# RWKV recurrence of a two-layer diffusion step: a product of 128 columns split into 64x64 parts, and a new order of the work

## The chip, the cores and the metric

The kernel runs on one core of a Trainium2 chip. A core has five engines that work in parallel, each through its own instructions in order: TensorE (PE, matrix products; PEld is its loading of weights), VectorE (DVE), ScalarE (ACT), GpSimd (POOL) and SyncE (SP), which here mostly issues DMAs. The metric is the device time of one execution in microseconds. Three runs of the kernel before gave 3995.91, 4006.51 and 4013.2 us; the median is 4006.51 us.

## The reference

One inference step over 128 context tokens and 2048 latent tokens of width 1024, in two layers. Layer 0 is Fourier mixing beside neighbourhood attention. Layer 1 is a bidirectional RWKV-7 mixer: 16 heads of 64, each with a 64x64 state, once forward and once backward, then a norm, a gate and an output projection. The recurrence is what the change touches:

```python
def step(S, inp):
    r_t, w_t, k_t, v_t, kk_t, a_t = inp
    sa = jnp.einsum('ebhvk,ebhk->ebhv', S, kk_t)
    S = (S * w_t[..., None, :] - sa[..., None] * (kk_t * a_t)[..., None, :]
         + v_t[..., None] * k_t[..., None, :])
    return S, jnp.einsum('ebhvk,ebhk->ebhv', S, r_t)
```

The output is the two token streams, the context keys and values of layer 0, and the final states of the context.

## The kernel before

The phases run one after the other: projections, Fourier mixing, attention and output of layer 0, projections of layer 1, then `phase_rwkv`, and `Final`, which norms, gates and projects row tiles of 128 tokens. The Tile framework derives the semaphores; in `phase_rwkv` the order of instructions on every engine is the order in which the program names them (`manual_schedule`).

The recurrence does not go token by token. It takes chunks of 64 tokens in a form with a triangular system per chunk and head. A **window** `w` (17 of them) holds four **units** `u`: two chunks forward (u = 0, 1) and two backward (u = 2, 3). Window 0 is the context. Eight pairs of heads lie in the tiles, one head in partitions 0 to 63, the other in 64 to 127 (`HF[0]`, `HF[1]`).

The work of a window is cut into 196 operations (some with instructions on one engine, the DMA ones on SP), named after small functions. `RW_PLAN` lists them once, each as `lag.name.arguments`; the loop at the end of `phase_rwkv` runs through this list again and again, and an entry with lag 3 works on the window three rounds back. So the list is one round of a software pipeline over up to five windows, and it sets the order on every engine's queue.

The operations that the prediction speaks of, with their engines and lines:

- `hl`, `ld`, `vl` (SP): loads of inputs; `ld` brings three tiles of 256 KB for a unit, `vl` the values. `st`, `sb` (SP): stores.
- `la` (PE, L1165), then `lt`, `lh`, `lf` (ACT, L1177, L1179, L1187, L1192): decay and rate.
- `sc` (DVE scan, L1201), `ew`, `ei` (ACT exponentials, L1205, L1209), `wc` (POOL, L1213).
- `fk`, `th_`, `bb`, `bk`, `xa`, `xr`, `fr` (DVE, L1218 to L1253): the tiles `BKb` (b and k) and `Xb` (r~ in columns 0 to 63, the other operand in 64 to 127). `bd` (SP, L1233): copies b of the upper heads beside their k, so that columns 64 to 191 of the upper half hold k and b.
- `ps` (PE): two loops. The first (L1265) makes [b k] x r~, the second (L1269) [b k] times the other operand. Each fills one of two buffers `pq` of PSUM, two banks each, that `la`, `ps`, `pt`, `pb`, `p1` and `p2` use in turn (`grab`).
- `dr` (DVE, L1276) masks the first result, `dx` (DVE, L1281) and `al` (ACT copy) take the second; `ad` (SP, L1295) moves halves of what `al` wrote. `pt` (PE transposes, L1303) with `at` (ACT); `pb` (PE, L1313) with `ab` (ACT).
- `tl` (DVE, L1327), 31 steps `td` (two DVE instructions each, L1339 and L1340), `tu`, `tt` (DVE, L1344, L1348), `tm` (POOL memset): the 32x32 triangles, inverted for a whole window at once. Then `uc` (ACT), `p1` (PE, L1360), `m1` (ACT), `p2` (PE, L1372), `uv` (ACT) put together the 64x64 inverses `UB`.
- per chunk `j` of the window and direction `e`: `RV` (PE, L1398), `R` (L1407), `rc` (ACT), `Z` (PE, L1426), `zc` (ACT), `S` (PE, L1442), `sa` (DVE sum into the state, L1447), `sm` (DVE decay of the state, L1455), and for the output `W_` (PE, L1419), `Y` (L1468), `yo` (ACT).

Arguments are the unit (`ps.3`) or chunk and direction (`sa.0.1`).

Three more tables hang other work into this order. `RW_FILL` says before which operations, counted from the first, steps of `z_gate` run: the second half of layer 1's gate product, 17 tiles of nine steps, 153 in all. `RW_LATE` is the operation before which the buffers of that product are given back. `RW_END` and `RW_TAIL` count from the end of the 3332 operations: at `RW_END` buffers are closed, and `RW_TAIL` says before which operations steps of `Final` run, `w` for loading and splitting the output weights (a split is one ACT and one DVE instruction a chunk), `t` for the first row tile, `u` for preparing the second.

Of the kernel before, what the change touches and what calls it, by code (L numbers as in the profile page):

```python
# [921 lines left out]
def z_gate(nc, g, hh, w, g2, zp, pp):  # L922
# [71 lines left out]


def phase_rwkv(tc, g, ins, outs, final):
# [23 lines left out]
    with ExitStack() as es:  # L1020
# [234 lines left out]
        def blocks(t):  # L1255
            return t.rearrange("p x (k t) -> p x k t", t=64)

        @op
        def ps(w, u):

            e, m, iW, t, f, BK, X = parts(w, u)
            o, q = blocks(grab(("ps", u, 0))), blocks(grab(("ps", u, 1)))
            for p in range(KC):
                for h in range(2):
                    nc.tensor.matmul(o[:, h, p], BK[HF[h], p, 64 * h:64 * h + 128], X[HF[h], p, 0:64], start=True, stop=True)  # L1265
            for p in range(KC):
                for x in range(2):
                    for h in range(2):
                        nc.tensor.matmul(q[HF[h ^ x], x, p], BK[HF[h], p, 64 * x:64 * x + 64], X[HF[h], p, 64:128],  # L1269
                                         start=True, stop=True)  # L1270
# [215 lines left out]
        with tc.manual_schedule():  # L1486
# [346 lines left out]
```

## Time and profile before

| | us |
|---|---|
| profiled execution, its time | 4006.46 |
| its span in the profile | 4004.7 |
| median of three runs | 4006.51 |
| PE busy, whole span | 3509.4 (88%) |
| DVE busy | 2597.0 (65%) |
| ACT busy | 1730.1 (43%) |
| POOL busy | 782.3 (20%) |
| first and last matmul of `ps` start | 2301.7, 3593.2 |

Times in the profile are microseconds from the start of the span. "Busy" counts the union of an engine's instructions, so a group of pipelined matmuls has a busy time far below its count times the duration of one. An idle time in a row is put down to what ended it last ("<-DVE OM L1276": the engine stood until that instruction had finished). The granted clock is the share of full speed that TensorE's throttle let through. A product of F32 operands appears as two matmul instructions.

### The profile page before, as it was taken

What the parts mean: (1) busy time and instruction counts of PE and PEld (TensorE: products, weight loads), DVE (VectorE), ACT (ScalarE), POOL (GpSimd) and SP (SyncE); (2) the same over time, 40 slices, a digit from 0 to 9 for tenths busy, and PEclk for the clock granted to TensorE, in tenths of its full rate; (3) what the DMA queues carried; (4) which work ended last, traced back from release to release, by engine and by line L of the source; (5) the groups of instructions that cost most, each with busy time, mean ns of one, the idle gap of its engine ahead of it and who ended that gap; (6) DMA issues with size and microseconds to landing.
All of it is one profiled execution on the core that took longest, in us unless ns stands there. A gap on an engine that the chain in (4) does not pass through costs nothing. (4 is left out here: it accounts for less than half of the span.)

```text
span 4004.7 us, 93003 instructions
## 1 busy us (share of the span) xinstructions
PE 3509.4 (88%) x39520; PEld 3039.7 (76%) x39520; DVE 2597.0 (65%) x4364; ACT 1730.1 (43%) x3629; POOL 782.3 (20%) x434
## 2 busy tenths in 40 slices
PE   6999998889999979999899997888888888885677
PEld 3999997567777769888687776877888778884555
DVE  6201101478867765899862347877878878875997
ACT  5110011266645533544442344555565555543444
POOL 3000000332202223323332320000000000001665
PEclk8999998999999989999899997788778888787888
DMA  6122214565546742434315542333233233224543
GB/s 213 64 71 86 69 58 139 159 172 143 135 121 191 186 111 81 135 103 115 119 67 153 157 122 79 88 92 86 78 92 86 78 92 98 76 76 152 202 165 115
DMA packets 514383, 463.07 MB, mean 116 GB/s; under 512 B 217111, under 2 KB 420391, under 8 KB 512430
## 3 DMA queue, kind: packets, MB, share of 16 engines
q1 hardware_dynamic: 506350, 444.95, 38.1%
q10 hardware_dynamic: 7616, 12.16, 0.9%
q8 instruction: 310, 5.08, 0.5%
q14 instruction: 107, 0.88, 0.1%
HBM read 314.13 MB, written 129.48 MB: 111 GB/s over the span
## 5 line engine op out<-in xcount | busy, mean ns | idle before, releaser
L34 POOL TENSOR_TENSOR xl<-xt,xh 128x1792 fp32r<-128x1792 f32 (+4 forms) x64 | 246.8, 3867 | 487.8 <-ACT xh L30 244.3
L40 PE MATMUL p<-ul,wh 128*128 128x436 f32 (+1 forms) x800 | 291.7, 365 | 2.4 <-DVE ul L34 2.1
L38 PE MATMUL p<-uh,wh 128*128 128x436 f32 (+1 forms) x800 | 291.5, 365 | 0.0
L39 PE MATMUL p<-uh,wl 128*128 128x436 f32 (+1 forms) x800 | 289.7, 362 | 0.0
L819 DVE SCALAR_TENSOR_TENSOR xt<-s,l1s,xt 128x448 f32<-128x448 f32 (+4 forms) x256 | 246.8, 1016 | 46.7 <-ACT xt L818 46.7
L834 PE MATMUL p<-xh,w 128*128 128x448 f32 (+2 forms) x640 | 240.4, 376 | 17.7 <-ACT w L30 10.2
L1213 POOL COPY WC<-W 128x8 f32<-128x8 f32 x68 | 29.8, 438 | 1133.4 <-DVE Sc L1455 671.4
L835 PE MATMUL p<-xh,w 128*128 128x448 f32 (+2 forms) x640 | 239.7, 374 | 0.0
L30 ACT ACTIVATE xh<-xt 128x1792 fp32r<-128x1792 f32 (+4 forms) x64 | 99.8, 1570 | 226.7 <-DVE xt L819 107.0
L1265 PE MATMUL pq<-Xb,BKb 64*128 64x64 f32 x2176 | 162.5, 304 | 37.6 <-DVE OM L1276 28.2
L1340 DVE TENSOR_TENSOR xe<-xe,l1s 128x31 f32<-128x31 f32 (+15 forms) x527 | 180.8, 343 | 18.1
L1339 DVE TENSOR_TENSOR l1s<-xe,xe 128x31 f32<-128x31 f32 (+15 forms) x527 | 179.6, 341 | 16.4
L1265 PEld LDWEIGHTS pq<-Xb,BKb 64*128 64x128 f32 x2176 | 151.2, 215 | 46.8 <-DVE OM L1276 31.0
L818 ACT ACTIVATE xt<-u,l1s 128x448 f32<-128x448 f32 (+4 forms) x256 | 142.0, 625 | 61.5 <-POOL xl L34 46.0
L40 PEld LDWEIGHTS p<-ul,wh 128*128 128x128 f32 x800 | 151.8, 190 | 12.6 <-DVE ul L34 4.5
L38 PEld LDWEIGHTS p<-uh,wh 128*128 128x128 f32 x800 | 151.9, 190 | 7.8 <-ACT uh L30 0.3
L39 PEld LDWEIGHTS p<-uh,wl 128*128 128x128 f32 x800 | 152.1, 190 | 7.5
L34 DVE TENSOR_TENSOR wl<-w,wh 128x2048 fp32r<-128x2048 f32 x12 | 27.5, 2291 | 189.5 <-ACT wh L30 189.5
L832 PE MATMUL p<-xl,w 128*128 128x448 f32 (+2 forms) x640 | 148.4, 369 | 1.1 <-POOL xl L34 1.1
L434 POOL TENSOR_TENSOR kl<-ld,kh 128x1088 fp32r<-128x1088 f32 x16 | 42.2, 2659 | 547.8 <-ACT kh L433 547.5
L834 PEld LDWEIGHTS p<-xh,w 128*128 128x128 f32 x640 | 123.6, 193 | 32.5 <-ACT w L30 11.1
L1303 PE MATMUL pq<-ident,BKb 64*128 64x64 f32 x1088 | 62.0, 256 | 92.0 <-DVE OM L1276 44.8
(375 smaller groups left out, 10036.9 us busy)
## 6 DMA issues: line engine op xcount, KB each, us to landing
x<-x SPq DMA_DIRECT2D x34, 512.0 KB
zu<-u1T SPq DMA_DIRECT2D x34, 512.0 KB
kk<-kkC SPq DMA_DIRECT2D x68, 256.0 KB
k<-kC SPq DMA_DIRECT2D x68, 256.0 KB
r<-rC SPq DMA_DIRECT2D x68, 256.0 KB
sv<-v SPq DMA_DIRECT2D x136, 128.0 KB
x<-in_x_sample SPq DMA_DIRECT2D x32, 512.0 KB
wmod<-in_ada_w SPq DMA_DIRECT2D x16, 1024.0 KB
```

Source lines behind the costliest of these rows:

```text
L34: (eng or nc.vector).tensor_tensor(lo, x, hi.bitcast(F32), op=ALU.subtract)
L38: nc.tensor.matmul(out, ah, bh, start=start, stop=False)
L39: nc.tensor.matmul(out, al, bh, start=False, stop=False)
L40: nc.tensor.matmul(out, ah, bl, start=False, stop=stop)
L818: nc.scalar.activation(x[:, j], us[hh][:, j, 1:n + 1], AF.Copy, scale=mu1[:, i, k:k + 1])
L819: nc.vector.scalar_tensor_tensor(x[:, j], ss[hh][:, j, :n], muh[:, i, k:k + 1], x[:, j], op0=ALU.mult, op1=ALU.add)
L832: nc.tensor.matmul(p[:, :n], w(wh, k), xl[:, k, :n], start=False, stop=(k == KC - 1))
L834: nc.tensor.matmul(p[:, :n], w(wh, k), xh[:, k, :n], start=(k == 0), stop=False)
L835: nc.tensor.matmul(p[:, :n], w(wl, k), xh[:, k, :n], start=False, stop=False)
L1265: nc.tensor.matmul(o[:, h, p], BK[HF[h], p, 64 * h:64 * h + 128], X[HF[h], p, 0:64], start=True, stop=True)
L1339: nc.vector.tensor_tensor(t, L[:, m:, j:m].to_broadcast([P, n, m]), Tm[:, j:m, :m].to_broadcast([P, n, m]), op=ALU.mult)
L1340: nc.vector.tensor_tensor(o, o, t, op=ALU.subtract)
```

## The change

The first loop of `ps` multiplied, for each pair of heads and each half, a stationary block of 64 rows and 128 columns (b and k side by side; the upper half starts 64 columns later, at k, so that its output rows come out as k, then b). Now it takes b and k apart as blocks of 64 columns and sends each to the half of the output where the 128-column form had put it. The numbers computed are the same. The order of the four products of a pair of heads goes over four combinations of row half and output half, as in the second loop. It no longer reads the columns that `bd` copies; `pt` still does.

The tables are replaced. All 196 operations are in both plans, and the plan has another starting point in its round (some operations that stood first with lag 4 now stand last with lag 3). `tl` stands last, with lag 2, in place of first, with lag 3. `RW_FILL` spreads its 153 steps up to operation 147 instead of 124.

```diff
--- before.py
+++ after.py
@@ -971,25 +971,25 @@
 
 
 RW_RINGS = 7, 6
-RW_FILL = {0: 20, 1: 1, 2: 1, 3: 1, 4: 1, 5: 1, 6: 1, 7: 2, 
...
-RW_END = -50
-RW_TAIL = {-50: 'wwtw', -46: 'w', -32: 'wwwwwttwtt', -31: 'twt', -30: 'ttw', -29: 't', -28: 'tt', -27: 'uw', -25: 'tt', -23: 'twtt', -22: 't', -20: 'uwt', -12: 'ttuwtttuwtt', -11: 'tuwt', -8: 'ttuwtttu', -2: 'tt'}
-RW_LATE = 126
+RW_FILL = {0: 20, 1: 1, 2: 1, 3: 1, 4: 1, 5: 1, 7: 1, 
...
+RW_END = -49
+RW_TAIL = {-29: 'wwtwwwwwwwttwtttwtt', -25: 'tw', -13: 'tttwutttwt', -12: 'ttwutttwutttwutttwut', -11: 'tt', -9: 'wutt', -1: 'tutt'}
+RW_LATE = 149
 RW_PLAN = """
-    3.tl 3.td.0 2.ei.1 4.rc.1.0 3.td.1 4.Z.1.0 4.yo.0.1 3.td.2 4.W_.1.0 3.td.3 3.td.4 3.td.5 4.rc.1.1 3.td.6 3.td.7
-    2.ps.0 3.td.8 3.td.9 3.td.10 4.Z.1.1 2.ld.2 4.zc.1.0 2.xr.1 2.al.0 4.Y.1.0 4.st.0.1 2.dr.0 4.W_.1.1 3.td.11 3.pt.3
-    2.dx.0 3.td.12 2.bk.1 4.st.0.0 2.bb.1 4.zc.1.1 4.Y.1.1 3.vl.0.0 2.fr.1 4.S.1.0 3.td.13 2.pt.0 4.yo.1.0 4.sa.1.0
-    3.RV.0.0 2.xa.1 3.at.3 2.ld.3 2.bd.1 3.td.14 3.td.15 4.S.1.1 2.ad.0 3.td.16 2.at.0 2.la.2.0 2.la.2.1 2.lt.2.0
-    2.lh.2.0 3.td.17 2.lt.2.1 4.sm.1.0 4.sa.1.1 3.RV.0.1 2.pt.1 2.lh.2.1 3.td.18 3.td.19 3.td.20 3.td.21 3.td.22
-    3.td.23 3.td.24 3.td.25 3.R.0.0 2.pb.1 2.at.1 2.wc.1 3.W_.0.0 3.vl.1.0 3.td.26 2.ab.1 3.td.27 3.td.28 3.td.29
-    1.hl.0 2.lf.2.1 3.td.30 3.tu 3.tt 2.ps.1 3.uc 3.sb.3 2.dr.1 2.sc.3 3.rc.0.0 2.lf.2.0 4.sm.1.1 3.p1 2.al.1 2.sc.2
-    2.ew.2 2.wc.2 2.dx.1 2.fk.3 3.m1 2.xr.2 2.xa.2 2.th_.2 3.R.0.1 4.yo.1.1 2.ei.2 2.th_.3 2.ew.3 3.p2 2.bb.2 2.ei.3
-    1.la.0.0 2.bb.3 2.bk.3 3.W_.0.1 2.wc.3 2.fk.2 3.rc.0.1 4.st.1.1 3.uv 1.lh.0.0 3.Z.0.0 2.bk.2 2.fr.2 1.lt.0.0
-    3.Z.0.1 3.zc.0.0 2.bd.3 2.ad.1 2.fr.3 2.xa.3 1.hl.2 2.xr.3 1.ld.1 2.pb.3 2.ab.3 1.la.0.1 1.ld.0 3.S.0.0 2.bd.2
-    3.sa.0.0 4.st.1.0 3.zc.0.1 2.pt.2 1.lt.0.1 1.sc.0 3.S.0.1 3.Y.0.1 3.vl.1.1 2.tm 3.sa.0.1 1.lh.0.1 2.at.2 3.RV.1.0
-    2.ps.3 1.ew.0 1.lf.0.1 3.RV.1.1 1.sc.1 1.lf.0.0 2.al.3 1.ei.0 3.sm.0.0 1.xr.0 1.xa.0 2.dx.3 2.dr.3 2.ps.2 1.th_.0
-    3.Y.0.0 3.R.1.0 2.al.2 1.fk.0 1.th_.1 2.ad.3 3.sm.0.1 1.fk.1 3.R.1.1 1.bb.0 1.wc.0 2.ad.2 1.bd.0 1.ew.1 1.bk.0
-    3.yo.0.0 2.vl.0.1 2.dx.2 2.sb.1 1.fr.0 2.dr.2
+    3.td.0 3.td.1 4.st.0.1 3.td.2 3.td.3 4.st.0.0 3.td.4 4.Y.1.0 3.td.5 3.at.3 3.td.6 2.ps.0 3.td.7 2.al.0 3.td.8
+    3.td.9 3.td.10 3.sb.1 4.yo.1.0 4.Y.1.1 2.dr.0 4.S.1.0 4.S.1.1 3.td.11 2.dx.0 3.td.12 3.vl.0.0 3.td.13 2.pt.0
+    4.sa.1.0 2.xa.1 2.bb.1 2.la.2.1 2.fr.1 3.td.14 3.td.15 2.at.0 3.td.16 3.td.17 3.RV.0.0 2.bd.1 2.la.2.0 3.td.18
+    2.lt.2.1 4.sm.1.0 2.xr.1 3.R.0.0 3.vl.0.1 3.W_.0.0 3.td.19 2.lh.2.1 3.rc.0.0 4.sa.1.1 3.sb.3 3.td.20 3.td.21
+    3.td.22 2.lh.2.0 3.td.23 3.td.24 2.pb.1 3.td.25 2.lt.2.0 2.ab.1 3.td.26 3.td.27 4.yo.1.1 3.td.28 3.vl.1.0 2.pt.1
+    2.at.1 3.td.29 3.td.30 3.tu 3.RV.0.1 3.tt 2.ps.1 2.tm 2.wc.1 2.dr.1 2.lf.2.1 4.sm.1.1 2.lf.2.0 2.ld.3 2.sc.2
+    2.al.1 3.uc 2.ld.2 2.ew.2 2.sc.3 3.p1 3.R.0.1 3.m1 2.ei.2 3.rc.0.1 2.th_.2 4.st.1.0 2.dx.1 2.xr.2 2.fk.2 2.wc.2
+    3.p2 2.ad.0 2.xa.2 2.ew.3 2.bk.2 2.fk.3 2.ei.3 2.th_.3 2.bb.3 1.la.0.0 2.wc.3 2.bb.2 3.W_.0.1 4.st.1.1 3.uv 2.fr.2
+    2.bk.3 3.Z.0.1 2.fr.3 3.Z.0.0 2.pb.3 1.lh.0.0 2.bd.2 1.lt.0.0 3.zc.0.1 2.xr.3 1.la.0.1 3.zc.0.0 2.ab.3 1.lt.0.1
+    2.xa.3 1.hl.2 3.S.0.1 1.ld.0 3.sa.0.1 3.S.0.0 2.bd.3 1.lh.0.1 3.sa.0.0 2.pt.2 1.sc.0 3.Y.0.1 2.at.2 3.RV.1.0
+    1.sc.1 3.sm.0.0 1.ew.0 1.ld.1 2.ps.3 2.ad.1 1.lf.0.1 3.vl.1.1 3.RV.1.1 1.xa.0 1.xr.0 1.wc.0 1.lf.0.0 2.dr.3 0.hl.0
+    2.dx.3 3.sm.0.1 1.th_.0 1.th_.1 2.al.3 1.ei.0 1.fk.0 2.ps.2 3.Y.0.0 3.yo.0.1 1.ew.1 1.fk.1 2.ad.3 2.dx.2 1.bb.0
+    2.al.2 3.R.1.1 2.ad.2 1.bd.0 3.yo.0.0 2.dr.2 3.rc.1.1 3.R.1.0 3.rc.1.0 1.bk.0 1.ei.1 3.Z.1.1 2.pt.3 3.Z.1.0 1.fr.0
+    3.W_.1.0 3.zc.1.0 3.zc.1.1 2.tl 3.W_.1.1 1.bk.1
 """
 
 
@@ -1261,8 +1261,9 @@
             e, m, iW, t, f, BK, X = parts(w, u)
             o, q = blocks(grab(("ps", u, 0))), blocks(grab(("ps", u, 1)))
             for p in range(KC):
-                for h in range(2):
-                    nc.tensor.matmul(o[:, h, p], BK[HF[h], p, 64 * h:64 * h + 128], X[HF[h], p, 0:64], start=True, stop=True)
+                for x in range(2):
+                    for h in range(2):
+                        nc.tensor.matmul(o[HF[h ^ x], h, p], BK[HF[h], p, 64 * x:64 * x + 64], X[HF[h], p, 0:64], start=True, stop=True)
             for p in range(KC):
                 for x in range(2):
                     for h in range(2):
```

More of the change, by code (lines that the diff above doesn't have):

```diff
@@ L973 @@
 RW_RINGS = 7, 6
-RW_FILL = {0: 20, 1: 1, 2: 1, 3: 1, 4: 1, 5: 1, 6: 1, 7: 2, 8: 1, 9: 1, 10: 1, 11: 1, 12: 1, 13: 1, 14: 1, 15: 1, 16: 1, 17: 1, 18: 1, 19: 1, 20: 1, 21: 2, 22: 1, 23: 1, 24: 1, 25: 1, 26: 1, 27: 1, 28: 1, 29: 1, 30: 1, 31: 1, 32: 1, 33: 1, 34: 1, 35: 2, 36: 1, 37: 1, 38: 1, 39: 1, 40: 1, 41: 1, 42: 1, 43: 1, 44: 1, 45: 1, 46: 1, 47: 1, 48: 1, 49: 2, 50: 1, 51: 1, 52: 1, 53: 1, 54: 1, 55: 1, 56: 1, 57: 1, 58: 1, 59: 1, 60: 1, 61: 1, 62: 1, 63: 2, 64: 1, 65: 1, 66: 1, 67: 1, 68: 1, 69: 1, 70: 1, 71: 1, 72: 1, 73: 1, 74: 1, 75: 1, 76: 2, 77: 1, 78: 1, 79: 1, 80: 1, 81: 1, 82: 1, 83: 1, 84: 1, 85: 1, 86: 1, 87: 1, 88: 1, 89: 1, 90: 2, 91: 1, 92: 1, 93: 1, 94: 1, 95: 1, 96: 1, 97: 1, 98: 1, 99: 1, 100: 1, 101: 1, 102: 1, 103: 1, 104: 2, 105: 1, 106: 1, 107: 1, 108: 1, 109: 1, 110: 1, 111: 1, 112: 1, 113: 1, 114: 1, 115: 1, 116: 1, 117: 1, 118: 2, 119: 1, 120: 1, 121: 1, 122: 1, 123: 1, 124: 1}
@@ L975 @@
-RW_END = -50
-RW_TAIL = {-50: 'wwtw', -46: 'w', -32: 'wwwwwttwtt', -31: 'twt', -30: 'ttw', -29: 't', -28: 'tt', -27: 'uw', -25: 'tt', -23: 'twtt', -22: 't', -20: 'uwt', -12: 'ttuwtttuwtt', -11: 'tuwt', -8: 'ttuwtttu', -2: 'tt'}
-RW_LATE = 126
+RW_FILL = {0: 20, 1: 1, 2: 1, 3: 1, 4: 1, 5: 1, 7: 1, 8: 1, 9: 1, 10: 1, 11: 1, 12: 1, 13: 1, 14: 1, 15: 1, 17: 1, 18: 1, 19: 1, 20: 1, 21: 1, 22: 1, 23: 1, 24: 1, 25: 1, 26: 1, 28: 1, 29: 1, 30: 1, 31: 1, 32: 1, 33: 1, 34: 1, 35: 1, 36: 1, 38: 1, 39: 1, 40: 1, 41: 1, 42: 1, 43: 1, 44: 1, 45: 1, 46: 1, 47: 1, 49: 1, 50: 1, 51: 1, 52: 1, 53: 1, 54: 1, 55: 1, 56: 1, 57: 1, 59: 1, 60: 1, 61: 1, 62: 1, 63: 1, 64: 1, 65: 1, 66: 1, 67: 1, 68: 1, 70: 1, 71: 1, 72: 1, 73: 1, 74: 1, 75: 1, 76: 1, 77: 1, 78: 1, 80: 1, 81: 1, 82: 1, 83: 1, 84: 1, 85: 1, 86: 1, 87: 1, 88: 1, 89: 1, 91: 1, 92: 1, 93: 1, 94: 1, 95: 1, 96: 1, 97: 1, 98: 1, 99: 1, 101: 1, 102: 1, 103: 1, 104: 1, 105: 1, 106: 1, 107: 1, 108: 1, 109: 1, 110: 1, 112: 1, 113: 1, 114: 1, 115: 1, 116: 1, 117: 1, 118: 1, 119: 1, 120: 1, 122: 1, 123: 1, 124: 1, 125: 1, 126: 1, 127: 1, 128: 1, 129: 1, 130: 1, 131: 1, 133: 1, 134: 1, 135: 1, 136: 1, 137: 1, 138: 1, 139: 1, 140: 1, 141: 1, 143: 1, 144: 1, 145: 1, 146: 1, 147: 1}
```

## The prediction

> **What bounds the kernel now.** I read the page first: TensorE is the busiest engine and the recurrence (L1265 and its neighbours) is its most broken-up stage. Then the stage by itself. A window of the recurrence begins with one VectorE transpose (`tl`, L1327), so its starts give the period.
>
> ```profile
> L1327 DVE STREAM_TRANSPOSE xe<-AF x17: 1917/1952/1973, 2415.3 to 3596.9; 128x1024 f32<-128x1024 f32 x17
> ```
> Seventeen starts, 16 intervals between 2415.3 and 3596.9: 73.85 us a window. Next the busy time by stretch: first the start up to the first `tl`, then window 0, then thirteen whole windows, then 103 us from the last `tl` on. The columns are stretch, length, busy us (instructions) of PE, PEld, DVE, ACT and POOL, granted clock, DMA share, GB/s.
>
> ```profile
> 2302.00:2415.30 113.30, 101.77 (x821) 78.64 (x820) 49.74 (x69) 44.59 (x94) 26.61 (x17) 0.95 0.42 117
> 2415.30:2488.90 73.60, 56.84 (x1164) 53.66 (x1166) 57.41 (x111) 36.41 (x82) 2.65 (x5) 0.67 0.24 66
> 2566.30:3526.20 959.90, 815.09 (x20395) 771.16 (x20391) 775.95 (x1469) 534.21 (x1171) 36.38 (x78) 0.83 0.31 87
> 3596.90:3700.00 103.10, 62.45 (x1289) 55.85 (x1284) 59.89 (x105) 38.73 (x75) 10.34 (x4) 0.73 0.47 143
> ```
> In the thirteen windows (73.84 us each) PE is busy 62.7 us a window, DVE 59.7, ACT 41.1, POOL 2.8. PE leads, yet idles 11.1 us a window and DVE 14.2; neither is full, so I ask who waits for whom. The waits of DVE over the same thirteen windows (us in total, times, longest):
>
> ```profile
> DVE Sc L1447 <- PE pz L1442: 113.0, 24, 8.0
> DVE Xb L1281 <- ACT AF L1134: 23.1, 13, 1.8
> DVE BKb L1228 <- issue: 7.9, 13, 2.1
> ```
> DVE waits 8.7 us a window for the sum into the state (`sa`, L1447), 1.8 for the mask of the second product (`dx`, L1281) and 0.6 before `bb`. One window's DVE, with the stalls in brackets, shows where:
>
> ```profile
> 2899.75 1.19 DVE L1276 TENSOR_TENSOR OM<-pq,masks 128x1024 f32<-128x1024 f32 x1
> ...
> 2920.49 0.69 DVE L1447 TENSOR_TENSOR Sc<-pz,Sc 128x512 f32<-128x512 f32 x1 [7.44 <-PE pz L1442]
> ...
> 2924.10 0.69 DVE L1447 TENSOR_TENSOR Sc<-pz,Sc 128x512 f32<-128x512 f32 x1 [1.52 <-PE pz L1442]
> ...
> 2929.79 0.69 DVE L1281 TENSOR_TENSOR Xb<-pq,masks 128x512 f32<-128x512 f32 x1 [1.78 <-ACT AF L1134]
> ...
> 2938.39 1.97 DVE L1327 STREAM_TRANSPOSE xe<-AF 128x1024 f32<-128x1024 f32 x1
> ```
> From its `tl` to the transpose before 2899.75 and on to the first `sa` DVE runs without a stall worth naming. It stands 7.44 us before that `sa`, 1.52 before the other direction's `sa`, 1.78 before `dx` of unit 3, and then works on to the next `tl`. So DVE's own row of work plus these three holes makes the period. What PE does in that stretch:
>
> ```profile
> 2894.02 3.36 PE L1265 MATMUL pq<-Xb,BKb 64*128 64x64 f32 x32
> 2897.32 1.98 PE L1269 MATMUL pq<-Xb,BKb 64*64 64x64 f32 x64
> 2900.99 3.62 PE L1360 MATMUL pq<-xe,AF 32*32 32x32 f32 x128 [1.69 <-DVE OM L1276]
> 2904.54 1.97 PE L1407 MATMUL pz<-Sc,Xb 64*64 64x64 f32 x32
> 2906.44 3.62 PE L1372 MATMUL pq<-UB,M 32*32 32x32 f32 x128
> 2909.99 2.08 PE L1165 MATMUL pq<-hb,wa 64*128 64x128 f32 x16
> 2912.00 1.97 PE L1419 MATMUL py<-Sc,Xb 64*64 64x64 f32 x32
> 2913.76 2.55 PE L1426 MATMUL pz<-R,UB 64*64 64x64 f32 x64
> 2916.24 1.96 PE L1313 MATMUL pq<-srk,f 128*128 128x16 f32 x16
> 2918.13 1.16 PE L1165 MATMUL pq<-hb,wa 64*128 64x128 f32 x16
> 2919.22 1.15 PE L1442 MATMUL pz<-sv,OM 128*64 128x64 f32 x32
> ...
> 2922.26 0.71 PE L1303 MATMUL pq<-ident,BKb 64*128 64x64 f32 x15 [1.69 <-DMA BKb<-BKb]
> ...
> 2926.00 2.00 PE L1265 MATMUL pq<-Xb,BKb 64*128 64x64 f32 x32
> 2927.93 1.16 PE L1269 MATMUL pq<-Xb,BKb 64*64 64x64 f32 x64
> ```
> The 7.44 us are a chain: the mask at 2899.75 frees the bank that `p1` (L1360) fills, then `p2` (L1372), `W_` (L1419), `Z` (L1426), `pb`, `la`, and `S` (L1442) at 2919.22, whose result `sa` adds. No `ps` is in that chain. The 1.52 us are the second `S` standing in PE's queue behind a transpose (`pt`, L1303) that waits 1.69 us for a DMA into BKb. The 1.78 us are `ps` of unit 3, 2926.00 to 2929.1, followed by ACT's copy (`al`), which L1281 waits for.
>
> **The matmuls.** Per unit 16 products of 64 rows x 128 columns become 32 of 64x64. F32 products count twice in the rows, so 32 instructions become 64, and in the run 2176 become 4352. The second loop of the same function already runs 4352 of 64x64 on the same four parts in the same order:
>
> ```profile
> L1265 PE MATMUL pq<-Xb,BKb 64*128 64x64 f32 x2176 | 162.5, 304 | 37.6 <-DVE OM L1276 28.2 <-DVE xe L1276 5.8 <-DMA BKb<-BKb 3.5
> ...
> L1269 PE MATMUL pq<-Xb,BKb 64*64 64x64 f32 x4352 | 95.1, 248 | 0.0
> ```
> Busy time per instruction: 162.5/2176 = 74.7 ns against 95.1/4352 = 21.9 ns. The new loop differs from the second one only in its banks and in which half of X moves, so I give it the second loop's 95.1 us: PE sheds 67.4 us in the run, 4.0 us a window. At the fast clock a unit goes from 2.00 to 1.16 us, at the slow one from 3.36 to 1.98. Bounds: from 95.1 (nearest row) up to 162.5 (if using both column halves of one bank from one row half cost what 128 columns cost).
>
> One rule speaks against that price. The Trainium skill (TensorE: Matmul & The Clock Gate, section "Wait — 56ns, not 53.3ns?") says that matmuls never start closer than about 25 ns, however short; by it, as an estimate, the new loop would take 109 us and the saving would be 54 us instead of 67. The trace disagrees: 64 of them take 1.16 us, 18 ns each.
>
> What of the 4.0 us lies on DVE's path? Only unit 3's `ps` ends a DVE hole, so at an unchanged order 0.84 of the 1.78 us goes; `ps` of unit 1 ends (2899.3) before its mask can begin anyway (2899.75, after a DVE transpose), and units 0 and 2 delay nobody. The rest becomes PE idle time.
>
> **The order.** I wrote out the new plan per engine, from `tl` round to `tl`.
>
> DVE: between `tl` and the transposes that end `td` the operations are the same ones (`xr.1` later, `bk.1` earlier). Between there and the first `sa` they are again the same nineteen. So the first hole, which is the chain above minus these nineteen, keeps its size if the chain does; in the chain PE still has `p1, R, p2, la, W_, Z, Z, pb, la, S`, only with direction 1 ahead of direction 0. I leave 7.44 as it is.
>
> After that: the two `S` now stand next to each other, and `pt.2` behind both; its DMA `bd.2` is issued on SP ahead of the six unit loads instead of behind them. The hole of 1.52 goes. The second `S` takes 1.15 us after the first, `sa` itself 0.69, so up to 0.5 of it may come back. The two scans follow both sums, covering `Y`, `RV` and `ps.3` on PE. Then `dr.3` comes before `dx.3`, and `al.3` after it. `dr.3` needs only the first, now shorter, half of `ps.3`, and `dx.3` starts a 1.2 us mask later, with no copy ahead of it: the hole of 1.78 goes. What is late next? `tl`, which waits for the last `ad` DMA; `al.2` now stands behind `yo.0.1` and `ew.1` on ACT, but `ps.2` starts earlier since its bank comes free with the earlier `dr.3`. I take no stall, with up to 1.8 (as much as the hole removed) as the bad end.
>
> Other queues: on SP `ld.2` and `ld.3` move behind the `td` stretch and their first users (`th_.2`, `fk.3`) come a few DVE operations behind; on POOL `wc.1` moves behind the memset `tm`, and `ew.2` waits for it; on ACT `lf.2.x` and `al.1` move ahead of `uc`. POOL has 2.8 us of work a window and ACT 41.1 of 73.8, so each has cover; without it `ew.2` would push the chain. PE receives `Z.1` and `pt.3` before `tl`, off DVE's path.
>
> Sum of a window: 1.5 + 1.8, plus half of the 0.6 before `bb`, which now has `dx.2` ahead of it: 3.6 us less, 70.2 us. Ends: 0.84 (only the shorter `ps`) and 5.0. Over 16 intervals: 58 us, ends 13 and 80.
>
> **Start.** The gate product of layer 1 fills PE there, nine steps a tile, in this spacing:
>
> ```profile
> 2290.24 1.02 PE L968 MATMUL pg<-zg,zs 128*128 128x512 f32 x2
> ...
> 2296.59 0.59 PE L968 MATMUL pg<-zg,zs 128*128 128x512 f32 x1
> ```
> 6.35 us a tile is 0.71 us a step. All 153 steps stand before the first `tl` now; 139 will. The other 14 (9.9 us) fall into window 0's `td`, where PE is busy 56.84 of 73.60 us: its 16.8 idle us hide them, and if that cover fails they cost their 9.9 there. With four `ps` at 0.84 the start sheds 13.3 us of PE work, and PE is 90% busy there (101.77 of 113.30). I take 10, ends 0 and 13.
>
> **End.** The output weights' first step moves from 50 to 29 operations before the last one, from about `p1` to after `RV.1.0`, some 21 us later (2904.5 to 2926 in the window shown). Five weight splits, each waiting for a load, now stand in DVE's queue ahead of the last window's `sm.0.1`; before, they and a row tile's first steps stood ahead of `sa.0.1`, so one detour replaces another. DVE idles 43 of the 103 us there, which covers a shift; I take 0, ends -10 and +21.
>
> Sum: 58 + 10 + 0 = 68 us off the profiled execution's own 4006.46 (its span of 4004.7 and 1.8 around it), which stands at the median of the runs, 4006.51: **3938 us**, with an own range of 3915 to 3965.
>
> **Rivals.**
> *PE bounds the window.* Its 85% is the largest share, and then all 67.4 us come off whatever the order: 3939 us. Against it: the largest DVE hole holds no `ps`. The time can't tell it from the forecast; the holes can. 0.06.
>
> *The first hole shrinks too.* In the window shown the chain ran mostly at the slow clock: `R` and `W_` take 1.97 us each, against 1.15 for the 32 instructions of L1442 at 2919.22, and the first `la` 2.08 against 1.16 for the second. With most of that gone, 2 us less in every window, 32 more: 3906 us. For it: the clock changes from window to window. Against: nothing in the edit touches that stretch. 0.09.
>
> *A new wait eats the order's gain.* `tl` waits for `ad.2`, or the second `sa` for PE, as much as now; only 0.84 us a window and the four `ps` of the start are left, 13 + 3 = 16 us: 3990 us. For it: every operation there is moved, and the queues are in order. 0.13.
>
> *The clock falls: slower.* Less PE work in the same period means more idle, and a lower clock: window 0 has PE busy 77% at clock 0.67, the thirteen 85% at 0.83. L1265's mean of 2.39 us a unit (162.5/68) lies 29% of the way from 2.00 to 3.36. So the changed PE work, 58.7 us a window, would be 48.8 at the fast clock and, 1.7 times that, 83 at the slow one. At half slow it is 66 us; with the 11.1 us that PE idles now, 77, 3.2 more than now, 51 in the run; less 10 at the start: 4047 us. It decides above 41% slow, where PE's work passes the present 62.7. Against it: with the period at 70.2 PE is 84% busy, as now. 0.07.
>
> The Trainium skill (the same page, section "Why this matters for your kernels") says that one window of idling of over about 3 us sends the array back to half clock. By that, too, longer PE holes would make this last case. The trace has stretches of both speeds, 3.36 and 2.00 us for the same 32 instructions, and does not show what starts them.
>
> **How the numbers follow.** Forecast 0.65, the rivals 0.06, 0.09, 0.13, 0.07. The range reaches from the deeper hole to the eaten gain: 3905 to 3988, leaving out the clock and about half of the eaten gain. A measurement of this kernel tells about 0.5%, 20 us, from no change. The eaten gain lies on that line, so of its 0.13 I count 0.05 as faster and 0.08 as same: faster 0.85, same 0.08, slower 0.07.
>
> **What would show it.** Right: L1269 and the new line near 95 us each; `tl` to `tl` about 70 us; DVE busy still 59.7 us a window; no DVE wait on `al` before L1281; `sa` waits about 7 us a window; the first `tl` about 10 us earlier after the gate's start. Wrong: a period of 72 us or more, a new wait before L1327 or L1447, the new loop above 130 us, or a granted clock under 0.75 over the windows.

## The result, and the profile after

The changed kernel takes 3897.79 us (median of 4 runs, 3897.04 to 3907.15), the one before beside it 4004.79: a ratio of 0.9738, 95% interval 0.9712 to 0.9765. A second measurement gave 3907.83 against 4007.06, 0.9752 (0.9731 to 0.9773). So the change takes 100 to 107 us off, where 68 were forecast; the first median lies 7 us below the range, the second 3 us inside it. The profiled execution took 3907.15 us (span 3905.3), and what follows is that one against the profiled one of before. Lines from L1266 on have moved by one.

The starts of `tl`:

```profile
L1328 DVE STREAM_TRANSPOSE xe<-AF x17: 1954/1972/2095, 2387.7 to 3499.2; 128x1024 f32<-128x1024 f32 x17
```
The 16 intervals take 1111.5 us, 69.5 each; before it was 1181.6. The first `tl` comes 27.6 us earlier, and from the last one to the end it is 406.1 us, before 407.8. The stretches again, in the columns of the prediction (start, window 0, thirteen windows, behind the last `tl`):

```profile
2274.40:2387.70 113.30, 107.76 (x1014) 82.50 (x1012) 63.33 (x78) 57.05 (x119) 35.44 (x20) 0.95 0.48 136
2387.70:2460.10 72.40, 56.49 (x1353) 50.50 (x1352) 60.68 (x117) 37.72 (x85) 2.33 (x6) 0.81 0.28 83
2536.90:3428.30 891.40, 727.48 (x22036) 687.48 (x22035) 772.28 (x1470) 540.51 (x1170) 39.48 (x78) 0.87 0.34 93
3499.20:3602.30 103.10, 60.15 (x1273) 54.08 (x1267) 57.95 (x105) 37.47 (x69) 10.35 (x4) 0.73 0.45 140
```
A window of the thirteen now takes 68.57 us, 5.27 less. DVE's own work is as it was, 59.4 us a window against 59.7. PE fell from 62.7 to 56.0 us, more than the 4.0 that its shorter loop sheds, since the granted clock rose from 0.83 to 0.87. What DVE still waits for in these windows (us in total, times, longest):

```profile
DVE Sc L1448 <- ACT lw L1177: 66.6, 10, 7.3
DVE Sc L1448 <- PE pz L1443: 10.3, 4, 3.5
DVE xe L1328 <- DMA AF<-AF: 5.0, 8, 1.5
DVE Sc L1448 <- ACT th L1187: 2.4, 10, 0.2
DVE Sc L1456 <- PE pz L1399: 2.0, 4, 1.3
DVE Xb L1282 <- PE pq L1270: 1.5, 3, 0.6
```
The waits before `sa` went from 113.0 to 79.3 us, those before `dx` from 23.1 to 1.5, those before `bb` (7.9) are no longer among the longest. `tl` waits longer for `ad`, 5.0 in place of 2.4, which is still small. (L1177 is an ACT operation that happens to end last; the chain is PE's, as before: in the windows shown, before and after, the first `sa` starts some 1.3 us after `S` does.) One window's DVE around the old holes:

```profile
2863.87 0.69 DVE L1448 TENSOR_TENSOR Sc<-pz,Sc 128x512 f32<-128x512 f32 x1 [7.03 <-ACT lw L1177]
2864.80 0.69 DVE L1448 TENSOR_TENSOR Sc<-pz,Sc 128x512 f32<-128x512 f32 x1 [0.24 <-ACT th L1187]
...
2869.45 1.21 DVE L1277 TENSOR_TENSOR OM<-pq,masks 128x1024 f32<-128x1024 f32 x1
2870.59 0.68 DVE L1282 TENSOR_TENSOR Xb<-pq,masks 128x512 f32<-128x512 f32 x1
...
2879.39 1.95 DVE L1328 STREAM_TRANSPOSE xe<-AF 128x1024 f32<-128x1024 f32 x1 [0.54 <-ACT lw L1209]
```
The second `sa` follows the first at once, and the mask `dr` goes straight into `dx`: the holes of 1.52 and 1.78 us are gone. The first hole is still there. Its chain on PE, in this window and then in one where it ran fast:

```profile
2844.74 3.63 PE L1361 MATMUL pq<-xe,AF 32*32 32x32 f32 x128 [4.51 <-DVE OM L1277]
2848.30 1.97 PE L1408 MATMUL pz<-Sc,Xb 64*64 64x64 f32 x32
2850.20 3.62 PE L1373 MATMUL pq<-UB,M 32*32 32x32 f32 x128
...
2862.60 2.08 PE L1443 MATMUL pz<-sv,OM 128*64 128x64 f32 x64
```

```profile
2572.46 2.21 PE L1361 MATMUL pq<-xe,AF 32*32 32x32 f32 x128 [0.72 <-DVE OM L1277]
2574.61 1.15 PE L1408 MATMUL pz<-Sc,Xb 64*64 64x64 f32 x32
2576.58 2.21 PE L1373 MATMUL pq<-UB,M 32*32 32x32 f32 x128 [0.83 <-DVE Xb L1282]
...
2586.61 2.08 PE L1443 MATMUL pz<-sv,OM 128*64 128x64 f32 x64
```
From `p1` to `S` it takes 17.86 us in the first and 14.15 in the second. The same two stretches up to the start of `sa`, in the columns of the stretches above:

```profile
2844.74:2863.87 19.13, 19.13 (x474) 18.44 (x476) 11.98 (x18) 12.45 (x26) 1.17 (x2) 0.66 0.39 114
2572.46:2587.87 15.41, 14.03 (x474) 13.37 (x476) 11.98 (x18) 12.87 (x27) 1.36 (x2) 1.00 0.31 80
```
The instructions and DVE's 11.98 us of work are the same; the granted clock is 0.66 in the first and 1.00 in the second. Over `p1` alone it is 0.50 (3.63 us) and 1.00 (2.21 us). In all 17 windows, the instructions of `p1` (ns min/median/max), before and after:

```profile
L1360 PE MATMUL pq<-xe,AF x2176: 191/236/258, 2449.3 to 3630.5; 32*32 32x32 f32 x198
```

```profile
L1361 PE MATMUL pq<-xe,AF x2176: 191/191/258, 2427.0 to 3532.7; 32*32 32x32 f32 x198
```
The median has moved from the slow value to the fast one. Over the thirteen windows the largest hole before an `sa` has a mean of 5.9 us, before 7.0. The two loops of `ps` in the run:

```profile
L1266 PE MATMUL pq<-Xb,BKb 64*64 64x64 f32 x4352 | 96.5, 232 | 7.3 <-issue 3.8 <-DVE OM L1277 2.1 <-DVE BKb L1238 1.3
L1270 PE MATMUL pq<-Xb,BKb 64*64 64x64 f32 x4352 | 92.0, 223 | 20.5 <-issue 20.0
```
The new loop takes 96.5 us, as forecast (95.1).

### The profile page after: what moved, and what is told of

Same layout as the page of the kernel before. It is cut to its first block, busy times and chain, and to the rows that moved or that the text cites. A ratio compares the mean times of both kernels' runs of the same rounds, so it can differ in the third digit from the quotient of the medians.

```text
span 3905.3 us, 97379 instructions
## 1 busy us (share of the span) xinstructions
PE 3387.4 (87%) x41696; PEld 2925.7 (75%) x41696; DVE 2591.3 (66%) x4364; ACT 1737.6 (44%) x3629; POOL 784.1 (20%) x434
## 5 line engine op out<-in xcount | busy, mean ns | idle before, releaser
L1408 PE MATMUL pz<-Sc,Xb 64*64 64x64 f32 x2112 | 97.3, 258 | 96.4 <-DVE Sc L1456 82.7
L1408 PEld LDWEIGHTS pz<-Sc,Xb 64*64 64x64 f32 x2112 | 87.8, 169 | 102.8 <-DVE Sc L1456 85.8
L1332 POOL MEMSET xe<- 128x1024 f32 x17 | 16.2, 952 | 684.7 <-DVE UB L1345 684.7
L30 ACT ACTIVATE wh<-w 128x2048 fp32r<-128x2048 f32 x12 | 22.9, 1911 | 251.3 <-PE p L40 157.5
```

The source lines that it names most:

```text
L1408: nc.tensor.matmul(pz[e][HF[h], p], X[HF[h], p, 64:128], Sc[e][HF[h], p], start=False, stop=True, skip_group_check=True)
```

## The experiments

Ratios are to the kernel before on the same chip, with 95% intervals; a per cent is 40 us. Holes and periods are means over the thirteen windows from the third `tl` on, in one profiled execution of each kernel; the first hole is the longest wait before an `sa` in a window.

**One part alone.** `ps_only`: the kernel before with the new loop. `order_only`: the changed kernel with the old loop.

```diff
-                for h in range(2):
-                    nc.tensor.matmul(o[:, h, p], BK[HF[h], p, 64 * h:64 * h + 128], X[HF[h], p, 0:64], ...)
+                for x in range(2):
+                    for h in range(2):
+                        nc.tensor.matmul(o[HF[h ^ x], h, p], BK[HF[h], p, 64 * x:64 * x + 64], X[HF[h], p, 0:64], ...)
```


> The 64x64 products alone, in the old order of the work (old plan, fill and tail). DVE's path sets the window: only the hole before dx of unit 3 shrinks, by 0.84 us of 1.78, so 16 x 0.84 = 13 us, and some 3 us at the start: 3988 us, a ratio of about 0.996, the period from 73.8 to 73.0 us, PE idle 4 us a window less busy. If PE bounded the window, all 67 us of shed PE work would come off: 3937 us, period 69.8.

> The new order (plan, fill, tail) with the old products of 128 columns. DVE's path: most of the gain is there; lost against the changed kernel are some 0.8 us a window where dx of unit 2 waits for ps, and 3 us at the start: about 3898 + 16 = 3914 us, period 69.4. If PE bounded the window: 3898 + 67 = 3965 us, period 72.6.

Measured: 3961.07 us, 0.9881 (0.9864 to 0.9898), and 3959.56 us, 0.9882 (0.9862 to 0.9903). Each alone takes 47 us off, and both expectations missed: the products give 27 us more than expected (and three times the 16 us of the "eaten gain" rival), the order 46 us less. The order's time lies near the 3965 of its rival that PE bounds the window, but the products' time does not fit the 3937 of the same rival. The two together, 100 to 107, are a little more than their sum of 94. DVE's waits with the old loop in the new order:

```profile
DVE Sc L1447 <- ACT lw L1177: 97.7, 13, 7.9
DVE OM L1276 <- PE pq L1265: 12.3, 10, 1.2
```
Here `dr` of unit 3 waits about 1 us a window for the longer `ps.3`, and no window has the short first hole (97.7/13 = 7.5 us). The granted clock in these windows is 0.78, where it was 0.83 before and is 0.87 in the changed kernel; the expectation had left that out. So in the new order the products are worth 3.0 us a window (71.56 to 68.57), 1.0 at `dr` and 1.6 in the first hole.

**Which units' products.** The old order, with the new loop for some units only (`ps_u3`, `ps_u012`, then `ps_u0`, `ps_u1`, `ps_u2`):

```diff
-                for h in range(2):
+                for x in range(2 if u == 3 else 0):
+                    ...
+                for h in range(0 if u == 3 else 2):
```


> Old order, 64x64 products for unit 3 alone. The prediction's step (only unit 3's ps ends a hole of DVE): 16 x 0.84 = 13 us and about 1 at the start, ratio 0.9965, which would leave the other 33 of the 47 us of the products alone unexplained. If the shorter ps of unit 3 also moves what follows it (its copy, ei, bb, the next ps): 20 to 30 us, 0.993 to 0.995.

> Old order, 64x64 products for units 0, 1 and 2, 128 columns for unit 3. The prediction's step (these three end no hole): only 3 us at the start, ratio 0.9993. If they shorten holes too (the second sum, bb, tl) or bring PE to the clock's change earlier: the missing 20 to 33 us, 0.992 to 0.995.

> The old order, with the 64x64 products for unit 0 only. Units 0, 1 and 2 together took 46 us off (0.9885), unit 3 alone 16, all four 47. Theory 1 (what matters is where the unit's ps stands): ps of unit 0 lies in the td stretch, in which DVE runs without a stall, so it takes next to nothing off the windows, at most the some 3 us of its share at the start: 0.998 to 1.000. Theory 2 (every unit's 0.84 us of PE work counts the same, since PE's queue holds everything up): a third of 46 us, 0.996. Rival of the prediction as it stood: nothing in the windows for units 0 and 2, 1.000.

> The old order, with the 64x64 products for unit 1 only. Its ps is the last PE work before the mask that frees the bank of p1, at the slow clock 3.36 + 1.98 us. Theory 1: in the windows where the mask waits for PE and not for DVE's transpose, the chain begins earlier; the two ended within 0.5 us of each other, so at most 0.5 us a window, 0.997 to 1.000, seen as an earlier p1 after the end of the td stretch. Theory 2 (all PE work counts the same): 0.996.

> The old order, with the 64x64 products for unit 2 only. Its ps stands behind that of unit 3, in front of Y, R and the copies that bb of the next window and the last dx wait for. Theory 1: the stretch from dx of unit 3 to dx of unit 2 (6.64 us before, 5.95 with units 0 to 2) shrinks by 0.7 us here, and the hole before bb goes: 0.7 to 1.2 us a window, 11 to 19 us, and most of the 46 us of units 0 to 2 is this one: 0.992 to 0.997. Theory 2 (all PE work counts the same): 0.996. The prediction as it stood: 1.000. Theory 1 is told from theory 2 by units 0 and 1, which have nothing by it.

| kernel | us | ratio (interval) | us off |
|---|---|---|---|
| ps_u3 | 3990.86 | 0.9961 (0.9947 to 0.9975) | 16 |
| ps_u012 | 3964.42 | 0.9885 (0.9865 to 0.9906) | 46 |
| ps_u0 | 3997.35 | 0.9972 (0.9957 to 0.9988) | 11 |
| ps_u1 | 3998.62 | 0.9977 (0.9960 to 0.9994) | 9 |
| ps_u2 | 3980.54 | 0.9937 (0.9915 to 0.9959) | 25 |

Unit 3 gives 16 us where 14 were expected, but units 0 to 2, costed at 3 us for the start and nothing in the windows, give 46, and over half of it is unit 2. In DVE's waits with unit 2 alone

```profile
DVE Sc L1450 <- PE pz L1445: 108.0, 26, 7.9
DVE Xb L1284 <- ACT AF L1134: 23.1, 13, 1.8
```
the `dx` row is untouched, the `sa` row is 5.0 us shorter, and `bb` (7.9 us before) has left the longest. From `dx` of unit 3 to `dx` of unit 2 DVE needs 5.95 us in place of 6.64, and the second `sa` comes 3.25 us behind the first in place of 3.82. For units 0 and 1 the intervals leave 2 to 17 us each. Theory 1 of these runs (the place of the unit decides) holds for unit 2; for 0 and 1 the runs are too alike to tell it from the second. Units 0, 1 and 2 add up (11, 9 and 25 for 46), but unit 3 does not add to them: 16 and 46 apart, 47 together.

**The order, undone in two places.** `undo_dx` puts unit 3's copy and masks back in the old sequence; `undo_S` puts a transpose between the two `S`, the DMA it waits for behind the loads, and the second `sa` behind a scan.

```diff
-2.dr.3 0.hl.0 2.dx.3 3.sm.0.1 1.th_.0 1.th_.1 2.al.3
+2.al.3 2.dx.3 2.dr.3 0.hl.0 3.sm.0.1 1.th_.0 1.th_.1
```

```diff
-1.lh.0.0 2.bd.2 1.lt.0.0 ... 1.hl.2 3.S.0.1 1.ld.0 3.sa.0.1 3.S.0.0 2.bd.3 1.lh.0.1 3.sa.0.0 2.pt.2 1.sc.0 ... 1.ew.0 1.ld.1
+1.lh.0.0 2.bd.3 1.lt.0.0 ... 1.hl.2 1.ld.1 1.ld.0 2.bd.2 3.S.0.1 3.sa.0.1 2.pt.2 3.S.0.0 1.lh.0.1 1.sc.0 3.sa.0.0 ... 1.ew.0
```


> The changed kernel with one place of the old order: al.3, then dx.3, then dr.3 behind ps.3. If this place is worth the hole that it had with the shorter products (0.95 us a window in the run of the products alone), 16 x 0.95 = 15 us slower than the changed kernel: about 3913 us, ratio 0.977 to 0.978, an L1282 hole of about 1 us a window. If the later work on DVE swallows it (tl waits for its DMA or PE anyway): no change, 0.974.

> The changed kernel with the other place of the old order: pt.2 between the two S, its DMA bd.2 behind the loads of two units, the second sa behind the first scan. If the second hole comes back (1.7 us a window before, 0.7 with the products alone): 12 to 28 us slower, about 3918 us, ratio 0.977 to 0.981. If the gain came from elsewhere: 0.974.

Measured: 3943.07, 0.9833 (0.9813 to 0.9853), and 3982.45, 0.9926 (0.9907 to 0.9946): 33 and 70 us of the gain given back (against 0.9752), where 15 and at most 28 were expected. The holes return where they were. First `undo_dx`, then `undo_S`:

```profile
DVE Xb L1281 <- ACT AF L1133: 18.9, 13, 1.7
```

```profile
DVE Sc L1447 <- ACT lw L1176: 91.0, 13, 7.4
DVE Sc L1447 <- PE pz L1442: 38.2, 13, 5.0
```
18.9/13 is 1.5 us a window before `dx`, 24 us in 16 intervals. The second hole is now 38.2/13 = 2.9 us, more than the 1.7 of before; the first rises to 7.0, and the one in `dx` stays away. Each of the two holes is thus tied to the entries that the prediction named. Undoing either also lengthens the first hole, by 0.7 and 1.1 us, which is 11 and 18 us in 16 intervals: part of what the expectations lacked.

**The tables.** `old_fill` has the old `RW_FILL` and `RW_LATE`, `old_tail` the tail steps of before, with its first two entries at -49 and -45. In `old_tail` the second row tile's inputs are read before the last of its rows are stored, so that part of this output is made from old values.

> The changed kernel with the old places of the gate product's steps (all 153 before the first tl) and of the giving back of its buffers. If the 14 steps that moved behind the first tl made the start shorter by their own 9.9 us of PE work: 3908 us, first tl 10 us later. If they made all of the 20 us that the start gained from the first la on: 3918. If the start gained by the plan's order alone: 3898.

> The changed kernel with the output weights' first steps as early as before (49 and 45 operations before the last) and the other tail steps at their old distances from the end. One detour for another, as the prediction had it: within 5 us of 3898. If the later start of the weights pays: 10 to 20 us slower; if it costs: as much faster.

Measured: 3914.21, 0.9758 (0.9736 to 0.9780), and 3910.87, 0.9757 (0.9740 to 0.9774), neither told from the changed kernel's 0.9752. In the profiles, from the first `la` to the first `tl` it is 121.5 us with the old fill against 117.3 and 115.3 in two of the changed kernel, so the later fill is worth some 4 to 6 us there. In `old_tail` the end, from the last `tl` on, takes 414.7 us against 406.2 and 405.6, and at most 409.9 in any other profile, so the later start of the weights seems to pay some 8 us there; shorter windows (68.3 us against 68.6) make up for part of it.

**The first hole.** Four runs on what is left, all on the changed kernel. `short_chain` takes `R.0.1` and `W_.0.1` out of the chain into PE's idle time before `p1` and puts `pb.3` behind `S`; `w_early` moves `W_.0.1` alone. (`sm.1.1` and `RV.0.1` go ahead of `tu` in both.)

```diff
 # short_chain
-3.tu 3.RV.0.1 3.tt 2.ps.1 2.tm ... 4.sm.1.1 ... 3.p1 3.R.0.1 3.m1 ... 2.bb.2 3.W_.0.1 ... 3.Z.0.0 2.pb.3 ... 3.sa.0.0 2.pt.2 ... 3.RV.1.0
+4.sm.1.1 3.tu 3.tt 2.ps.1 3.R.0.1 3.W_.0.1 2.tm ... 3.p1 3.m1 ... 2.bb.2 ... 3.Z.0.0 ... 3.sa.0.0 3.RV.1.0 ... 2.pb.3 2.ab.3 2.pt.2
```


> The changed kernel with a shorter chain behind the first hole: R and W_ of direction 1 go ahead of p1 into PE's idle time there (sm.1.1 goes ahead of tu), pb.3 goes behind the two S. If the first hole is that chain on PE: about 4 us less from p1 to the first S, of which some 2 us a window are left after the next waits: 16 x 2 = 32 us faster than the changed kernel, 3866 us, ratio about 0.966. If something else sets the hole (the loads, ACT): 0.974.

> The changed kernel with W_.0.1 moved from between p2 and Z to ahead of p1, where PE stands idle for some 5 us; RV.0.1 and sm.1.1 move ahead of tu for it. All else stays, so unlike the kernel with the shorter chain nothing is put in front of ps of unit 3. Theory (the first hole is PE's own row p1 to S): the row loses 1.97 us at the slow clock, 1.15 at the fast one; the first hole goes from 5.9 us to some 4.2, the period from 68.6 to some 67, 25 to 30 us in the run: 0.968. Rival: S waits for ACT's uv and zc anyway, so PE idles in place of W_: 0.975, as the changed kernel, with a hole of 5.9. Second rival: the scan sc or the mask dr is late in its place, as in the shorter chain: 0.978 or more.

Both missed: 3935.54, 0.9813 (0.9795 to 0.9831), and 3914.99, 0.9774 (0.9748 to 0.9800). The shorter chain did cut `p1` to `sa` from 18.0 to 15.3 us and the first hole from 5.9 to 3.7, but made a new wait:

```profile
DVE OM L1276 <- PE py L1468: 34.3, 11, 4.9
DVE Sc L1447 <- PE pz L1442: 27.7, 20, 4.8
```
`dr` of unit 3 now stands for its `ps` (the row names the last product by the clock, a `Y` right behind `ps.3`), which `pb.3` and `pt.2` have been put in front of. In `w_early` nothing is put there, and the hole still only falls to 5.7. The chain itself, from `p1` to `sa`, falls only from 18.0 to 17.3 us, for a reason that depends on the clock. In a window in which PE had the full clock, it is ACT:

```profile
2583.56 2.21 PE L1372 MATMUL pq<-UB,M 32*32 32x32 f32 x128 [0.23 <-DVE Xb L1281]
2585.70 1.16 PE L1164 MATMUL pq<-hb,wa 64*128 64x128 f32 x16
2587.55 0.33 PE L1426 MATMUL pz<-R,UB 64*64 64x64 f32 x2 [0.69 <-ACT UB L1133]
2588.59 2.07 PE L1426 MATMUL pz<-R,UB 64*64 64x64 f32 x62 [0.71 <-ACT UB L1133]
```

```profile
2586.51 2.04 ACT L1133 ACTIVATE UB<-pq 32x1024 f32<-32x1024 f32 x2
```
`Z` (L1426) stands twice for ACT's two copies of `UB`, which can only follow `p2`. From the end of `p2` to `S` it is 7.81 us, the same as in the fast window of the changed kernel, although `W_` has gone: the chain has a second strand on ACT, as the first rival of that run has it. In a slow window it is the clock:

```profile
2864.26 3.25 PE L1426 MATMUL pz<-R,UB 64*64 64x64 f32 x64
```
This `Z` starts at once behind `la`, in the place of `W_`, and so still within the slow stretch: the granted clock over it is 0.64, where it was 0.93 over the 2.17 us of `Z` behind `W_` in the changed kernel. And `sm.1.1`, 0.6 us of DVE's work that had stood behind the mask and covered part of the chain, is now ahead of `tu`: DVE's own row there falls from 13.3 to 12.8 us, so that of the 0.7 us only 0.2 reach the hole. In its new place `sm` waits, 0.8 us a window for all of them in place of 0.2.

`busy_gaps` fills PE's idle time with repeated products, to keep the clock up; its expectation undercounts them, they are 240 more a window. `dense_p` has 96 products of 64x64 on four parts in place of the 64 of 32x32, each in `p1` and `p2`, to see whether that shape brings on the slow clock; its inverses lack their off-diagonal part.

```diff
 # busy_gaps
-            for j in range(4):
+            for j in range(16 if (u, hf) == (2, 0) else 4):
+                j %= 4
 # and the second loop of ps
-            for p in range(KC):
+            for p in range(KC * (4 if u == 1 else 1)):
+                p %= KC
```

```diff
 # dense_p, in p1 and in p2 alike
-            for x in range(32):
-                for q in (0, 64):
-                    nc.tensor.matmul(o[q + 32:q + 64, x], a[q:q + 32, 1, x], TD[q:q + 32, x], ...)
+            for p in range(3 * KC):
+                p %= KC
+                for x in range(2):
+                    for h in range(2):
+                        nc.tensor.matmul(d[HF[h ^ x], x, p], X[HF[h], p, 64:128], Sc[1][HF[h], p], ...)
```


> The changed kernel with repeated products that write the same values again, in PE's two idle gaps of some 4.5 us (la.2.0 four times instead of once ahead of R.0.0; the second loop of ps.1 four times ahead of p1): 42 instructions of window work more of PE, nothing less to do. In the changed kernel slow stretches of PE begin right behind these gaps, and the first hole is 3.3 us where the chain ran fast and about 7.2 where slow. If the gaps bring on the slow clock: the hole is 3.3 to 4 us in all windows, 2 to 2.6 us less than its mean of 5.9, 30 to 40 us faster, about 3862 us, ratio 0.965, granted clock over 0.9 in the windows. If the clock is set by something else: the extra work is covered, 0.974, or costs what is not covered, 0.98.

> The changed kernel with other products in the place of p1 and p2: 96 of 64x64 on the four parts each instead of 64 of 32x32 (64 of a state with X; the copies behind them multiply by zero, so the inverses lack their off-diagonal part, and states and outputs are not the reference's). If the 32x32 products bring on the slow clock in the chain: from the end of p2 to S 7.8 us in all windows, as in the fast windows of the changed kernel, against 8.2 to 9.5 in its slow ones, and no slow stretch from 38 us after tl on. If they don't: slow stretches there as before.

Measured: 3943.58, 0.9837 (0.9819 to 0.9855), and 3934.57, 0.9817 (0.9796 to 0.9838). The windows of `busy_gaps`:

```profile
2545.20:3463.50 918.30, 776.02 (x25181) 732.36 (x25178) 773.78 (x1469) 537.24 (x1171) 35.12 (x78) 0.91 0.33 91
```
The granted clock does rise, 0.91 against 0.87, and yet PE has it in full from `p1` to `sa` in only two of the 13 windows, and the first hole is 6.9 us. That is not the clock alone: in five windows `p1` itself had the full clock and still took 3.0 to 3.9 us. In `dense_p` the new `p1` takes 3.03 us in five windows, at a granted clock of 1.00 and with PE idle for 1.3 to 1.7 us ahead of it, and 4.3 or more in six, at 0.50 to 0.67 and with 4.3 to 5.6 us of idle time. So the slow clock comes to these products as well: the 32x32 shape does not bring it on. But it goes sooner. These slow stretches last 3.4 to 6.8 us, where those at `p1` in the changed kernel last 10.2 to 13.7, and `p2` has a granted clock of 1.00 in all thirteen windows, where it has 0.50 in eight of the changed kernel. What `p1` and `p2` consist of does matter for how long the slow clock lasts; whether by shape or by amount, this run does not tell.

`after_again` is the changed kernel once more.

> The changed kernel once more, beside the next three on the same chip: a ratio within 0.001 of 0.974, first hole near 5.9 us on the mean with some windows at 3.3.

Measured: 3907.83, 0.9752, as told above; its windows take 68.64 us and its first hole 5.6.

## Why the prediction was wrong in size and right in kind

**Right.** DVE's holes set the window, and its own work did not change. The second hole and the one before `dx` went, each by the entries named. (All three were sized from one window, 7.44, 1.52 and 1.78 us; the means of the thirteen are 7.0, 1.7 and 1.8.) The new loop costs 96.5 us for 95.1. The end is worth 1.7 us for 0. `tl` waits about 0.5 us a window, well inside the 1.8 left for it. The rival of a falling clock is out (0.83 to 0.87 in the windows), and so is the one of the eaten gain. That PE bounds the window is out as well: the products shed 67 us of PE's work and alone bring 47, and the order brings as much with PE's work unshed.

**Wrong by 31 us in the profiled execution** (3938 to 3907), which splits into the 16 intervals (70 for 58), the start (20 in its own stages for 10), 7.6 us that the unchanged stages ahead of the recurrence were faster in this execution, and 1.7 at the end: 12 + 10 + 7.6 + 1.7 = 31. The start of the first `la`, then of the gate product, before and after:

```profile
L1165 PE MATMUL pq<-hb,wa x1088: 272/272/578, 2278.0 to 3548.4; 64*128 64x128 f32 x182
L968 PE MATMUL pg<-zg,zs x68: 590/592/1057, 2157.5 to 2409.6; 128*128 128x512 f32 x68
```

```profile
L1165 PE MATMUL pq<-hb,wa x1088: 266/272/580, 2270.4 to 3445.1; 64*128 64x128 f32 x182
L968 PE MATMUL pg<-zg,zs x68: 590/592/1061, 2149.8 to 2399.6; 128*128 128x512 f32 x68
```
Both begin some 7.6 us earlier, ahead of anything that the change touches; that much is one execution against another. From the first `la` to the first `tl` it is 117.3 us for 137.3.

**The step that failed: "so the first hole ... keeps its size if the chain does ... I leave 7.44 as it is."** The chain did not keep its size. From `p1` to `sa` its mean went from 19.0 to 18.0 us, while DVE's own row beside it stayed at 13.3, so the first hole fell from 7.0 to 5.9. In three windows of the thirteen the granted clock was 1.00 over the whole chain, which then took 15.4 to 15.6 us and left a hole of 3.3 to 3.5. In three more only `p1` was fast: in one the clock fell to 0.50 right behind it, in two `p2` stood for 1.5 us for nothing that the profile shows. In the other seven the clock over the chain was 0.65 to 0.71, as in every window of before (0.62 to 0.72).

This is not an accident of one execution. Four profiles have both the new plan and the new products: the changed kernel twice, `old_fill` and `old_tail`. In them three, four, seven and six windows had the full clock over the whole chain, and the first hole was 5.9, 5.6, 4.9 and 5.5 us. In the eight profiles with the old plan, or with the old products in the new plan, no window had, and the hole was 7.0 to 7.5.

So the first hole gave 1.1 us a window, 14 us in the thirteen: the rival "the first hole shrinks too" happened in about half its size, and its counter-argument, that nothing in the edit touches that stretch, was the mistake. The edit touches what runs ahead of it. Why the clock then stays up in some windows and not in others is left open (see the last section). The hole before `bb` went whole (0.6 for 0.3); the wait of `tl` took some 0.3 back. In sum the thirteen windows gave 5.27 us each, 1.7 more than the 3.6 forecast, or 22 us; the first two windows and the last gave 1.6 us together where the forecast had 11. That makes the 12 above.

**The split was wrong too.** "Units 0 and 2 delay nobody" was read off the first and third hole alone. Unit 2's `ps` lies between the `dx` of units 3 and 2, and its length shows in the small wait before `bb`, which the prediction put down to the order, and before the second `sa`: some 12 us of the thirteen windows. In the forecast of the whole this hardly counted, since the order removes the same holes; the expectation for the products alone was 27 us short by it.

**The start** was costed as PE work moved away: 13.3 us, of which 10 was taken. It gave 20. From the first `la` to the first `tl` PE was busy 125.8 of 137.3 us and is now busy 111.8 of 117.3. So 14.0 us of work went, as costed, and 6.0 us of PE's idle time, which had no term. `old_fill` puts 4 to 6 us of the 20 down to the later fill.

## What to carry to other kernels

Cost each stall of the engine that sets the period, and also the chain behind the largest one at both clocks: where the same instructions are seen at two durations, the hole has two sizes, and an edit ahead of it can change how often each comes. Before calling a shorter instruction free, look at every wait of the limiting engine in the stretch behind it, small ones too, not just the two or three largest. And of a chain with copies between its products, shortening one engine's strand shows only until the other's is the longer.

## What the runs showed of the hardware

**Two clocks in one chain.** 128 instructions of 32x32 took 2.21 us where the granted clock was 1.00 and 3.62 where it was 0.50; 32 of 64x64 took 1.15 or 1.97. In the changed kernel `p1` ran fast (2.21 to 2.27 us) in the six windows in which PE had idled 0.6 to 1.1 us just before it. It ran slower (3.0 to 3.6 us) in the other seven: in six of them PE had idled 3.2 to 5.0 us, in the seventh only 1.75. The two quoted windows, 0.72 and 4.51 us, are of each kind. The pauses depend on each other: in every window a slow stretch also begins around PE's idle time before `R.0.0`, 4.6 us in most. Where that stretch lasts 13.7 us, `ps.1` ends later, `p1` follows soon, and `p1` is fast; these are the six. Where it lasts 3.4 to 10.2 us, PE pauses again before `p1`, and the next slow stretch meets `p1`.

The Trainium skill (TensorE: Matmul & The Clock Gate, section "Why this matters for your kernels") says that one window of over about 3 us of idling sends the array back to half clock; the two quoted windows agree with that. So do all 18 profiles: PE has 251 idle times of 3.5 us or more in their thirteen windows, and the slow clock was on at the end of every one or came on within 3.5 us. But no such gap is needed. In `busy_gaps` PE was idle nowhere as long as 2.5 us, and 18 slow stretches still begin in the thirteen windows. Nor does a slow stretch end when the gap is over: in eleven windows of `order_only` one lasts 30.7 us, from the idle time before `R.0.0` through `ps.1`, `p1` and `p2`, although PE had no idle time just before `p1`. So idling of that length is enough here but not needed, and what else starts a slow stretch, and what ends it, is left open.

**The price of a small product.** 64 instructions of 64x64 on four parts in turn take 1.16 us, 18 ns each, and 128 of 32x32 take 2.21 us, 17 ns. The Trainium skill (TensorE: Matmul & The Clock Gate, section "Wait — 56ns, not 53.3ns?") gives a floor of about 25 ns between starts; counted by recorded instructions both are below it. Counted by products, each of which is two of these instructions, they are above it: 36 and 35 ns.
